# Placing F32R weight parts, activations and tiles at fixed distances from multiples of 256 bytes in SBUF

## The chip, the cores and the metric

The kernel runs on one core of a Trainium2 chip. The metric is the device time of one execution in microseconds; the time before is 1332.7 us, the median of 3 runs (1332.43 to 1333.14).

## The reference, cut to what matters

Two transformer blocks over 256 tokens of width 1024, all in float32.

```python
# block 1: adaLN modulation, top-k attention beside a short convolution, then PEER
mod = silu(c) @ w_ada + b_ada                    # shift1, scale1, gate1, shift2, scale2, gate2
h = rms_norm(x, norm1_w) * (1 + scale1) + shift1
proj = h @ w_in                                  # q k v | conv b c x | indexer q k w
y_mix = concat(rms_norm(dsa_attention(...)), rms_norm(short_conv(...)))
x = x + gate1 * (y_mix @ w_out)
h2 = rms_norm(x, norm2_w) * (1 + scale2) + shift2
# peer_ffn: 8 heads, 2 x 128 sub-keys, 16 of 16384 experts per head and token
a = gelu(einsum('qhkd,qd->qhk', peer_u[expert], h2))
x = x + gate2 * einsum('qhk,qhkd->qd', g * a, peer_v[expert])
# block 2, two layers: window attention and chunked gating, two gated branches, layer_norm
h = x @ w_in[l] + b_in[l]
merged = sigmoid(g_a) * (y_a @ w_branch_attn[l]) + sigmoid(g_g) * (y_g @ w_branch_gmlp[l])
x = layer_norm(ALPHA * x + merged @ w_out[l] + b_out[l], ln_g[l], ln_b[l])
```

## The kernel before

**Precision.** Most products are made of three F32R matmuls: an operand is split into a high part (a copy rounded to F32R) and a low part (what is left), and `mm3` (lines 245 to 248) adds high x high, high x low and low x high into one PSUM tile. `split` (lines 224 to 233) does it for a weight slab of 128 x 1024: ScalarE writes `wh` (L229), VectorE writes `wl` (L232). Slabs come with `load` (L219 to 222), 512 KB a DMA on the queue of SyncE. The slabs `w`, `wh`, `wl` have three buffers each, all in the pool `wpool`. Where plain F32 is enough, `load_any` puts a slab into any of these buffers and the matmul uses it whole.

**Stationary and streaming.** The first operand of a matmul is loaded as weights (PEld), the second streams (PE). In `mm_block` the weight slab is loaded and 256 columns of activations stream; in `mm_rows`, `rows_tile` and `v_mm` activations (or z parts) are loaded and 512 columns of the slab stream. Each matmul of the trace has a weight load of its own.

**Stages.** First stage: projections, attention and convolution, out projection, queries. U stage (`u_block`, 128 blocks): scores of all experts, each block 24 matmuls with `h2h`, `h2l`; the gelu goes into `Z`. Between the blocks a generator (`steps`) hands out the top-16 searches and then the `gates`, which build one-hot products in F16 and multiply `Z`; a budget of `STEP` = 1.45 per block sets how much of it is issued after each block. V stage (lines 1052 to 1080): for each of 128 slabs of `v`, `split_x` splits `Z[:, j]` into `zh`, `zl` (L241, L242), and `v_mm` (L1017) issues twelve matmuls of 512 columns into four PSUM tiles that stay open. At j = 80 `gate2_rows` makes eight small diagonal tiles `gdiag` (two buffers; L1038) that TensorE uses at L1039. Second block: `proj2` (24 matmuls of 256 columns with `xh4`, `xl4`), branch projections with `yh`, `yl`, rows with `mm_rows` and `rows_tile` (L1117), the latter from slabs split ahead into the buffers of sga, sgg, yh, yl (`wfirst`, `wlast`) or of ygT, yaT4.

**Order.** Each engine works its queue in order. Tiles are placed by stacks of pools: one grows from the low end of SBUF, a second, `using_default_side("right")`, from the high end (`gx`, later `xh4`, `xl4`). A tile is put right behind the one before it, at the next multiple of 32 bytes. In the program as built from the kernel before, these are the start addresses modulo 256 (each buffer of a tile has the same one):

| tile | start mod 256 |
|---|---|
| ident, the first tile of all | 128 |
| w, wh, wl | 160 |
| hh, hl (first stage) | 0 |
| h2h, h2l (U), Z, zh, zl (V), yh, yl, sga | 160 |
| xh4, xl4 | 224 |
| mh, ml, gx | 192 |

Slices in these tiles are whole multiples of 256 bytes apart (128 columns are 512 bytes), so a matmul's operands have the residue of their tiles.

Of the kernel before, what the change touches and what calls it, by code (L numbers as in the profile page):

```python
# [9 lines left out]
F32 = mybir.dt.float32  # L10
F32R = mybir.dt.float32r
F16 = mybir.dt.float16
# [7 lines left out]
P = 128  # L20
T = 256
D = 1024
# [9 lines left out]
BIG = -1e38  # L32
MARK = -3e38
WB = 3
EARLY = 2
STEP = 1.45
PRI = 300
# [124 lines left out]

def build(tc, d, out):
    nc = tc.nc
    ctx = ExitStack()
    V, S, G, TE = nc.vector, nc.scalar, nc.gpsimd, nc.tensor

    def pool(name, bufs, st=ctx, space=None):  # L170
        kw = {"reuse_waits": "tile"}
        if space is not None:
            kw["space"] = space
        return st.enter_context(tc.tile_pool(name=name, bufs=bufs, **kw))

    cst = pool("cst", 1)
    res = pool("res", 1)
    wpool = pool("wpool", 4)
    psm = pool("psm", 4, space=PSUM)


# [9 lines left out]
    def cc(name, i=0, n=1):  # L191
        o, w = COLS[name]
        return cols[:, o + i:o + i + n]
# [17 lines left out]
    def nm(s):  # L211
        uid[0] += 1
        return f"{s}_{uid[0]}"
# [3 lines left out]


    def load(src):  # L219
        w = wpool.tile([P, 1024], F32, tag="w", name=nm("w"), bufs=WB)  # L220
        nc.sync.dma_start(w, src)
        return w

    def split(w, hi=S, lo=V, dst=None):
        if dst is None:
            dst = [wpool.tile([P, 1024], F32R, tag=t, name=nm(t), bufs=3) for t in ("wh", "wl")]
        wh, wl = dst
        if hi is S:
            S.activation(wh, w, AF.Copy)  # L229
        else:  # L230
            hi.tensor_copy(wh, w)
        lo.tensor_sub(wl, w, wh.bitcast(F32))  # L232
        return wh, wl

    def split_x(pl, src, shape, name, hi=V, lo=V):
        xh = pl.tile(shape, F32R, tag=name + "h", name=nm(name + "h"))
        xl = pl.tile(shape, F32R, tag=name + "l", name=nm(name + "l"))
        if hi is S:
            S.activation(xh, src, AF.Copy)
        else:  # L240
            hi.tensor_copy(xh, src)  # L241
        lo.tensor_sub(xl, src, xh.bitcast(F32))  # L242
        return xh, xl
# [12 lines left out]

    def load_any(src, i):

        w = wpool.tile([P, 1024], (F32, F32R, F32R)[i], tag=("w", "wh", "wl")[i], name=nm("wn"), bufs=3)
        w = w if i == 0 else w.bitcast(F32)  # L260
        nc.sync.dma_start(w, src)
        return w
# [17 lines left out]
    def psum_mm():  # L280
        return psm.tile([P, 512], F32, tag="mm", name=nm("psmm"))
# [45 lines left out]
    st1 = ExitStack()  # L327
    psa = pool("psa1", 4, st1, PSUM)
    p1 = pool("p1", 1, st1)
    pw = pool("pw", 2, st1)  # L330
    adap = pool("adap", 5, st1)
    stg = ExitStack()
    with tc.using_default_side("right"):
        pg = pool("pg", 1, stg)
# [2 lines left out]
        return psa.tile([P, 512], F32, tag="aux", name=nm("aux"))  # L337

    xT = p1.tile([P, NCH, T], F32, name="xT")
    c1 = p1.tile([1, D], F32, name="c1")  # L340
    oc = ROWS["c"][0]
    nc.sync.dma_start(c1, d["rows"][0:1, oc:oc + D])
    xrow = p1.tile([P, 2, D], F32, tag="sq", name="xrow")
# [27 lines left out]
    def ada_col(dst, b, w, pl, crow):  # L371

        junk = pl.tile([P, D], F32, tag="junk", name=nm("junk"), bufs=1)
        V.scalar_tensor_tensor(junk, w, 0.5, crow, ALU.mult, ALU.mult, accum_out=dst)  # L374
        if b is not None:
            V.tensor_add(dst, dst, b)
# [25 lines left out]
    for k in range(NCH):  # L402
        ad = [ada_load(), ada_load()]
        wa = load(d["wa"][k])
        wb = p1.tile([P, D], F32, tag=("yaT", "ccT")[k % 2], name=nm("wb"))
        nc.sync.dma_start(wb, d["wb"][k])
# [14 lines left out]
        f, e = k == 0, k == NCH - 1  # L421
# [30 lines left out]
    def nload():  # L452
        w = load_any(d["w1"][wi[0]], wi[0] % 3)
        wi[0] += 1
        return w
# [19 lines left out]
    ada_step(5)  # L475


    iqT = p1.tile([P, 4, T], F32, name="iqT")
    for i in range(2):
        S.activation(iqT[:, 2 * i:2 * i + 2], iqp[i], AF.Copy)  # L480
    ikT = p1.tile([P, T], F32, name="ikT")
# [159 lines left out]
    for hp in range(4):  # L641
        ps = aux()
        for q in range(2):
            h = 2 * hp + q
# [17 lines left out]

    outp = []
    gx = pg.tile([P, NCH, T + 1], F32, name="gx")

    def out_half(half, y):

        for g in range(4):
            w = nload()
            if half == 0:  # L670
                ada_step(2)
                outp.append(psum_mm())
            for q in range(2):
                ps = outp[g][:, q * T:(q + 1) * T]
                for k in range(4):
                    sl = slice((4 * q + k) * P, (4 * q + k + 1) * P)
                    TE.matmul(ps, w[:, sl], y[:, k], start=half == 0 and q == 0 and k == 0, stop=half == 1 and k == 3,  # L677
                              skip_group_check=True)
            if half == 1:
                with tc.high_priority(offset=PRI):  # L680
                    for q in range(2):
                        n = 2 * g + q
                        V.scalar_tensor_tensor(x1T[:, n], outp[g][:, q * T:(q + 1) * T], gate1[:, n:n + 1], xT[:, n],
                                               ALU.mult, ALU.add)
                        S.activation(sq[:, n], x1T[:, n], AF.Square)
                        V.tensor_scalar(gx[:, n, :T], x1T[:, n], cw2[:, n:n + 1], None, ALU.mult)
# [39 lines left out]
    qps = []  # L726
    for s in range(EARLY):
        w = nload()
# [6 lines left out]
                        token_sum(ps2[:, :2], sq[:, n], n, NCH)  # L735
        qps.append(ps)
    powed = []
    rs2 = res.tile([P, T], F32, name="rs2")
    with tc.high_priority(offset=PRI):
        rs2p = rstd_bcast(pw, ps2[:, :2], D, EPS, aux, powed)  # L740
        V.tensor_copy(rs2, rs2p)
# [5 lines left out]
    Z = zp.tile([P, NJ, T], F32, name="Z")  # L747
# [55 lines left out]
    def retrieval_query(s):  # L803

        q2 = q2s[s % 3]
        if s < EARLY:
            qb = pu.tile([P, 1], F32, tag="qb", name=nm("qb"), bufs=2)
# [176 lines left out]
    for j in range(NJ):  # L984
# [3 lines left out]
        while budget > 0:  # L988
            c = next(todo, None)
# [6 lines left out]

    stv = ExitStack()
    psv = pool("psv", 1, stv, PSUM)
    pv = pool("pv", 3, stv)
    with tc.using_default_side("right"):  # L1000
        p4x = pool("p4x", 1)
    xr = x1T.rearrange("p k t -> p (k t)").rearrange("p (t d) -> p t d", t=2)
    xh4 = p4x.tile([P, NCH, T], F32R, name="xh4")
    xl4 = p4x.tile([P, NCH, T], F32R, name="xl4")

    acc = [psv.tile([P, 512], F32, name=f"vacc{i}") for i in range(4)]
    crow2 = pv.tile([P, D], F32, name="crow2", bufs=1)
# [5 lines left out]
    def v_mm(j, i, wh, wl, zh, zl):  # L1013

        ts_, sl = slice(i // 2 * P, (i // 2 + 1) * P), slice(i % 2 * 512, (i % 2 + 1) * 512)
        for n, (a, b) in enumerate(((zh, wh), (zh, wl), (zl, wh))):
            TE.matmul(acc[i], a[:, ts_], b[:, sl], start=j == 0 and n == 0, stop=j == NJ - 1 and n == 2)  # L1017

    def x1_rows():

        ps = [psum_mm() for _ in range(4)]
        for i in range(4):
            t, hf = i // 2, i % 2
            for q in range(4):
                TE.transpose(ps[i][:, q * P:(q + 1) * P], x1T[:, 4 * hf + q, t * P:(t + 1) * P], ident)
        for i in range(4):
            S.activation(xr[:, i // 2, i % 2 * 512:(i % 2 + 1) * 512], ps[i], AF.Copy)

    def gate2_rows():

        g2s = pv.tile([P, 8], F32, name="g2s", bufs=1)
        V.tensor_add(g2s, modB[:, 24:32], cc("bada", 40, 8))
        V.tensor_scalar(g2s, g2s, 1.0 / WSCALE, None, ALU.mult)
        for hf in range(2):
            ps = psum_mm()
            for q in range(4):
                dg = pv.tile([P, P], F32, tag="gdiag", name=nm("gdiag"), bufs=2)
                V.tensor_scalar(dg, ident, g2s[:, 4 * hf + q:4 * hf + q + 1], None, ALU.mult)  # L1038
                TE.matmul(ps[:, q * P:(q + 1) * P], ones, dg, start=True, stop=True)  # L1039
            S.activation(crow2[:, hf * 512:(hf + 1) * 512], ps, AF.Copy)  # L1040
# [11 lines left out]
    held = []  # L1052
    for j in range(NJ):
        if j % 8 == 4 and adai[0] < 48:
            ada_col(modB[:, adai[0] - 16:adai[0] - 15], None, load(d["ada"][adai[0]]), pv, crow2)
            adai[0] += 1
        w = load(d["v"][j])
        held.append(split(w) + split_x(pv, Z[:, j], [P, T], "z"))
        if j < NJ - VTAIL:
            for i in range(4):  # L1060
                v_mm(j, i, *held[-1])
            held.pop()
        if j == 16:
            x1_rows()
        if j == 80:
            gate2_rows()
    for i in range(4):
        for n, h in enumerate(held):
            v_mm(NJ - VTAIL + n, i, *h)
        t, sl = i // 2, slice(i % 2 * 512, (i % 2 + 1) * 512)  # L1070
# [14 lines left out]
    st4 = ExitStack()  # L1085
    psa = pool("psa4", 4, st4, PSUM)
    p4 = pool("p4", 1, st4)
    pq = pool("pq", 2, st4)
    w2i = [0]

    def next2():
        w = load(d["w2"][w2i[0]])
        w2i[0] += 1
        return w

    def split2(w, dst=None):
        return split(w, dst=dst)
# [36 lines left out]
    for l in range(2):  # L1134
        xh, xl = xh4, xl4
# [167 lines left out]
        for b in range(4):  # L1303
            ps = aux()
            for q in range(2):
                h = b + 4 * q
# [17 lines left out]
        for n in range(NCH):  # L1324
            wh, wl = split2(next2())
            pa = psum_mm()
            mm_block(pa[:, :T], wh, wl, yh, yl, n=4)
            pg = psum_mm()
# [74 lines left out]
```

## Time and profile before

| | |
|---|---|
| profiled execution | 1332.5 us |
| its span | 1330.3 us |
| PE busy | 1305.5 us, 98% |
| PEld busy | 1187.7 us, 89% |
| DVE busy | 1025.1 us, 77% |
| ACT busy | 631.0 us, 47% |
| DMA | 254.85 MB, mean 192 GB/s |

A matmul's busy time is from its start to its modelled end, and the next one starts well before that; the distance from start to start is what a matmul costs. In the chain of waits a piece of PE is exactly that distance. The granted clock is a share of full speed: 1.00 is 2.4 GHz.

### The profile page before, as it was taken

What the parts mean: (1) busy time and instruction counts of PE and PEld (TensorE: products, weight loads), DVE (VectorE), ACT (ScalarE), POOL (GpSimd) and SP (SyncE); (2) the same over time, 40 slices, a digit from 0 to 9 for tenths busy, and PEclk for the clock granted to TensorE, in tenths of its full rate; (3) what the DMA queues carried; (4) which work ended last, traced back from release to release, by engine and by line L of the source; (5) the groups of instructions that cost most, each with busy time, mean ns of one, the idle gap of its engine ahead of it and who ended that gap; (6) DMA issues with size and microseconds to landing.
All of it is one profiled execution on the core that took longest, in us unless ns stands there. A gap on an engine that the chain in (4) does not pass through costs nothing.

```text
span 1330.3 us, 23463 instructions
## 1 busy us (share of the span) xinstructions
PE 1305.5 (98%) x8968; PEld 1187.7 (89%) x8968; DVE 1025.1 (77%) x2159; ACT 631.0 (47%) x1100; POOL 21.1 (2%) x35
## 2 busy tenths in 40 slices
PE   7999999999999999999999999999989999999997
PEld 6868899999999999999888888888869999899996
DVE  7899399984688889885777777777784867868676
ACT  5535154644555544444443343343344754457642
POOL 1000000000000000000000000000010000000000
PEclk8999999999999999999999999999999999999999
DMA  9896244555544454545766776555665465554653
GB/s 369 317 345 233 84 144 150 167 191 187 172 165 159 148 167 147 173 158 187 224 202 218 216 221 201 180 191 194 196 232 160 142 222 187 189 174 140 209 191 111
DMA packets 72545, 254.85 MB, mean 192 GB/s; under 512 B 8305, under 2 KB 10481, under 8 KB 72178
## 3 DMA queue, kind: packets, MB, share of 16 engines
q1 hardware_dynamic: 72434, 253.36, 57.6%
q8 instruction: 71, 1.16, 0.3%
q14 instruction: 40, 0.33, 0.1%
HBM read 252.28 MB, written 1.05 MB: 190 GB/s over the span
## 4 chain that ended last, share of the span: by engine, by line
PE 88%; DVE 9%; ACT 1%; issue 1%; DMA 0%; DVEq 0%; POOL 0%; SPq 0%; POOLq 0%
PE vacc L1017 25%; PE psmm L246 15%; PE psmm L248 14%; PE psmm L247 14%; PE psmm L1117 3%; PE aux L955 2%; PE psmm L677 2%; DVE wl L232 2%; PE aux L443 2%; PE psmm L463 1%; PE iqp L443 1%; DVE Z L826 1%; PE aux L1207 1%; DVE junk L374 1%; PE psr L246 1%
## 5 line engine op out<-in xcount | busy, mean ns | idle before, releaser
L229 ACT ACTIVATE wh<-w 128x1024 fp32r<-128x1024 f32 x373 | 394.6, 1060 | 484.5 <-PE psmm L247 207.9
L232 DVE TENSOR_TENSOR wl<-w,wh 128x1024 fp32r<-128x1024 f32 x373 | 455.5, 1222 | 182.1 <-ACT wh L229 179.5
L246 PE MATMUL psmm<-h2h,wh 128*128 128x256 f32 x1136 | 327.7, 288 | 0.0
L248 PE MATMUL psmm<-h2h,wl 128*128 128x256 f32 x1136 | 322.4, 284 | 3.6 <-DVE wl L232 3.6
L247 PE MATMUL psmm<-h2l,wh 128*128 128x256 f32 x1136 | 321.0, 283 | 0.0
L248 PEld LDWEIGHTS psmm<-h2h,wl 128*128 128x128 f32 x1136 | 217.1, 191 | 5.8 <-DVE wl L232 5.5
L247 PEld LDWEIGHTS psmm<-h2l,wh 128*128 128x128 f32 x1136 | 217.3, 191 | 0.2 <-DVE h2l L774 0.2
L246 PEld LDWEIGHTS psmm<-h2h,wh 128*128 128x128 f32 x1136 | 217.1, 191 | 0.0
L1017 PE MATMUL vacc<-wh,zh 128*128 128x512 f32 x512 | 199.6, 390 | 0.0
L1017 PE MATMUL vacc<-wh,zl 128*128 128x512 f32 x512 | 199.5, 390 | 0.0
L1017 PE MATMUL vacc<-wl,zh 128*128 128x512 f32 x512 | 199.2, 389 | 0.0
L246 PE MATMUL psmm<-xh,wh 128*128 128x256 f32 x544 | 154.2, 283 | 0.0
L248 PE MATMUL psmm<-xh,wl 128*128 128x256 f32 x544 | 151.9, 279 | 0.0
L247 PE MATMUL psmm<-xl,wh 128*128 128x256 f32 x544 | 151.6, 279 | 0.0
L1017 PEld LDWEIGHTS vacc<-wh,zl 128*128 128x128 f32 x512 | 96.1, 188 | 20.1 <-DVE zl L242 0.2
L1017 PEld LDWEIGHTS vacc<-wl,zh 128*128 128x128 f32 x512 | 96.1, 188 | 19.8
L1017 PEld LDWEIGHTS vacc<-wh,zh 128*128 128x128 f32 x512 | 96.1, 188 | 19.8
L246 PEld LDWEIGHTS psmm<-xh,wh 128*128 128x128 f32 x544 | 102.1, 188 | 0.9 <-ACT yh L1316 0.3
L248 PEld LDWEIGHTS psmm<-xh,wl 128*128 128x128 f32 x544 | 102.2, 188 | 0.7 <-DVE mx L1218 0.7
L247 PEld LDWEIGHTS psmm<-xl,wh 128*128 128x128 f32 x544 | 101.9, 187 | 0.1
L242 DVE TENSOR_TENSOR zl<-Z,zh 128x256 fp32r<-128x256 f32 x128 | 54.6, 427 | 13.2 <-DVE zh L241 0.5
L947 DVE TENSOR_TENSOR oh<-iohr,ij 128x1024 f16<-128x1024 f16 x64 | 44.2, 693 | 22.8 <-PE aux L955 21.6
(388 smaller groups left out, 1732.0 us busy)
## 6 DMA issues: line engine op xcount, KB each, us to landing
w<-u SPq DMA_DIRECT2D x128, 512.0 KB, 3.3
w<-v SPq DMA_DIRECT2D x128, 512.0 KB, 4.2
w<-w SPq DMA_DIRECT2D x122, 512.0 KB, 3.8
ada<-ada SPq DMA_DIRECT2D x40, 512.0 KB, 6.1
wn<-w SPq DMA_DIRECT2D x23, 512.0 KB, 5.9
w<-wa SPq DMA_DIRECT2D x8, 512.0 KB, 7.5
wb<-wb SPq DMA_DIRECT2D x8, 512.0 KB, 4.8
w<-ada SPq DMA_DIRECT2D x8, 512.0 KB, 4.1
```

What stands on the lines that cost most here:

```text
L229: S.activation(wh, w, AF.Copy)
L232: lo.tensor_sub(wl, w, wh.bitcast(F32))
L242: lo.tensor_sub(xl, src, xh.bitcast(F32))
L246: TE.matmul(ps, sh, mh, start=first, stop=False)
L247: TE.matmul(ps, sh, ml, start=False, stop=False)
L248: return TE.matmul(ps, sl, mh, start=False, stop=last).ins
L443: TE.matmul(ps, st, mv, start=first, stop=e and part == 1, skip_group_check=True)
L677: TE.matmul(ps, w[:, sl], y[:, k], start=half == 0 and q == 0 and k == 0, stop=half == 1 and k == 3, skip_group_check=True)
L947: V.tensor_tensor(oh, bc(iohr.unsqueeze(1), [P, 4, P, 2]), bc(ij.unsqueeze(2), [P, 4, P, 2]), ALU.is_equal)
L955: TE.matmul(o, oh[:, i, :, q % 2], ow[:, i + r, :, q % 2], start=r == 0, stop=r == 1)
L1017: TE.matmul(acc[i], a[:, ts_], b[:, sl], start=j == 0 and n == 0, stop=j == NJ - 1 and n == 2)
L1117: last_mm[0] = TE.matmul(ps, x[:, k, ts_], slabs[k // 2][part][:, sl], start=k == 0 and r == 0 and i == 0, stop=k == NCH - 1 and r == 1).ins
```

## The change

Every SBUF pool is wrapped in `Lines`: a tile whose bytes per partition are no multiple of 256 is allocated with the next multiple and a view of it returned; tiles under 256 bytes of a pool that has `small` go to a pool of small tiles. `placed` opens two pools behind gaps of 64 and 128 bytes and a third gap of 64 behind them: `wh` goes to the first, `wl` to the second, three buffers each. The V stage gets two such pools for `zh` and `zl`. `edge` adds 96 bytes to a pool of the high side. Beside that, `c1` gets the buffer of `iqT`, `rs2` moves to the pool of `gx`, and `gdiag` has one buffer in place of two.

```diff
+LINE = 256
+HI_AT, LO_AT = 64, 192
+class Lines:
+    def edge(self):
+        self.pool.tile([P, 24], F32, name=self.name + "_edge")
+    def tile(self, shape, dtype, **kw):
+        size = 2 if dtype is F16 else 4
+        n = int(np.prod(shape[1:]))
+        if n * size % LINE == 0:
+            return self.pool.tile(shape, dtype, **kw)
+        if n * size < LINE and self.small is not None:
+            return self.small.tile(shape, dtype, **{"bufs": self.bufs, **kw})
+        t = self.pool.tile([shape[0], -(-n * size // LINE) * LINE // size], dtype, **kw)[:, :n]
...
+    def placed(name, st=ctx, bufs=3):
+        out, at = [], 0
+        for i, to in enumerate((HI_AT, LO_AT, 0)):
+            if (to - at) % LINE:
+                gap = st.enter_context(tc.tile_pool(name=f"{name}gap{i}", bufs=1))
+                gap.tile([P, (to - at) % LINE // 4], F32, name=f"{name}gap{i}")
+            at = to
+            if i < 2:
+                out.append(pool(f"{name}{i}", bufs, st))
+        return out
-    wpool = pool("wpool", 4)
+    wpool = pool("wpool", WB)
+    parts = placed("wpart")
-            dst = [wpool.tile([P, 1024], F32R, tag=t, name=nm(t), bufs=3) for t in ("wh", "wl")]
+            dst = [p.tile([P, 1024], F32R, tag=t, name=nm(t)) for p, t in zip(parts, ("wh", "wl"))]
-    def split_x(pl, src, shape, name, hi=V, lo=V):
-        xh = pl.tile(shape, F32R, tag=name + "h", name=nm(name + "h"))
-        xl = pl.tile(shape, F32R, tag=name + "l", name=nm(name + "l"))
+    def split_x(pls, src, shape, name, hi=V, lo=V):
+        xh = pls[0].tile(shape, F32R, tag=name + "h", name=nm(name + "h"))
+        xl = pls[1].tile(shape, F32R, tag=name + "l", name=nm(name + "l"))
+    p1.small = pw.small = pool("small", 1, st1).pool
-    c1 = p1.tile([1, D], F32, name="c1")
+    c1 = p1.tile([1, D], F32, tag="iqT", name="c1")
-    iqT = p1.tile([P, 4, T], F32, name="iqT")
+    iqT = p1.tile([P, 4, T], F32, tag="iqT", name="iqT")
+    pg.edge()
-    rs2 = res.tile([P, T], F32, name="rs2")
+    rs2 = pg.tile([P, T], F32, name="rs2")
-    pv = pool("pv", 3, stv)
+    pv = pool("pv", 2, stv)
+    pz = placed("z", stv)
+    p4x.edge()
-                dg = pv.tile([P, P], F32, tag="gdiag", name=nm("gdiag"), bufs=2)
+                dg = pv.tile([P, P], F32, tag="gdiag", name=nm("gdiag"), bufs=1)
-        held.append(split(w) + split_x(pv, Z[:, j], [P, T], "z"))
+        held.append(split(w) + split_x(pz, Z[:, j], [P, T], "z"))
+    p4.small = pq.small = pool("small4", 1, st4).pool
```

## Rows read from the trace of the kernel before

**Rows 1.** Page, part 1: busy time, share of the span, instructions.
```profile
PE 1305.5 (98%) x8968; PEld 1187.7 (89%) x8968; DVE 1025.1 (77%) x2159; ACT 631.0 (47%) x1100; POOL 21.1 (2%) x35
```
**Rows 2.** Page, part 4: the chain by engine.
```profile
PE 88%; DVE 9%; ACT 1%; issue 1%; DMA 0%; DVEq 0%; POOL 0%; SPq 0%; POOLq 0%
```
**Rows 3.** Table of stretches: busy PE, PEld, DVE, ACT, POOL; granted clock, DMA share, GB/s.
```profile
0.00:60.00 60.00, 53.30 (x293) 46.02 (x294) 50.34 (x99) 28.84 (x42) 4.10 (x11) 0.94 0.96 363
...
172.00:285.00 113.00, 109.37 (x889) 106.88 (x888) 112.25 (x478) 59.90 (x94) 0.00 (x0) 1.00 0.50 161
288.00:345.00 57.00, 57.00 (x478) 57.00 (x477) 26.95 (x25) 27.00 (x43) 0.00 (x0) 1.00 0.60 194
440.00:540.00 100.00, 100.00 (x936) 98.84 (x936) 89.55 (x168) 50.69 (x118) 0.00 (x0) 1.00 0.49 159
```
**Rows 4.** Chain, 310 to 312.6 us: start, us, what; first and last of 22.
```profile
309.98 0.12 PE psmm L248
...
312.50 0.12 PE psmm L248
```
**Rows 5.** Chain, 1191.5 to 1194.3 us; first and last of 25.
```profile
1191.43 0.12 PE psmm L248
...
1194.26 0.12 PE psmm L248
```
**Rows 6.** Chain, 1169.1 to 1171.8 us; first and last of 24 of 256 columns.
```profile
1169.14 0.12 PE psmm L246
...
1171.75 0.11 PE psmm L248
```
**Rows 7.** Chain of the whole execution: long pieces of PE.
```profile
137.51 14.25 PE psmm L677 x66
...
677.29 174.14 PE vacc L1017 x768
...
1143.99 11.20 PE psmm L1117 x48
```
**Rows 8.** Groups of weight loads, 288 to 345 us: count, busy us, mean ns, idle before.
```profile
L246 PEld LDWEIGHTS psmm<-h2h,wh 128*128 128x128 f32 x159 | 30.5, 192 | 0.0
```
**Rows 9.** Groups of weight loads, 1111 to 1143 us.
```profile
L246 PEld LDWEIGHTS psmm<-yh,wh 128*128 128x128 f32 x60 | 11.5, 192 | 0.0
```
**Rows 10.** Groups of weight loads, 1171 to 1185 us.
```profile
L246 PEld LDWEIGHTS psmm<-xh,wh 128*128 128x128 f32 x42 | 7.9, 188 | 0.0
```
**Rows 11.** Tile yh: count, ns least/median/most, first and last start.
```profile
L246 PE MATMUL psmm<-yh,wh x128: 277/283/290, 1109.6 to 1299.9; 128*128 128x256 f32 x128
```
**Rows 12.** Table of stretches, instructions with h2h (first two rows), with h2l (last two).
```profile
285.00:345.00 60.00, 60.00 (x335) 51.98 (x335) 0.00 (x0) 0.00 (x0) 1.00 0.59 193
345.00:629.00 284.00, 265.36 (x1393) 220.47 (x1391) 0.00 (x0) 0.00 (x0) 1.00 0.50 162
...
285.00:345.00 60.00, 47.14 (x168) 32.02 (x167) 0.00 (x0) 1.00 0.59 193
345.00:629.00 284.00, 196.50 (x696) 132.95 (x696) 0.00 (x0) 1.00 0.50 162
```
**Rows 13.** Instructions of DVE in order, 440 to 447 us: start, us.
```profile
440.98 0.69 DVE L947 TENSOR_TENSOR oh<-iohr,ij 128x1024 f16<-128x1024 f16 x1 [0.39 <-PE aux L955]
441.59 1.22 DVE L232 TENSOR_TENSOR wl<-w,wh 128x1024 fp32r<-128x1024 f32 x1
...
444.38 0.69 DVE L947 TENSOR_TENSOR oh<-iohr,ij 128x1024 f16<-128x1024 f16 x1 [0.38 <-PE aux L955]
```
**Rows 14.** Page, part 5: matmuls of xh in the second block.
```profile
L246 PE MATMUL psmm<-xh,wh 128*128 128x256 f32 x544 | 154.2, 283 | 0.0
```
**Rows 15.** Groups of matmuls, 1169.5 to 1185 us.
```profile
L246 PE MATMUL psmm<-xh,wh 128*128 128x256 f32 x47 | 13.0, 276 | 0.0
```
**Rows 16.** Instructions in order, 849 to 857 us: gdiag and its matmuls.
```profile
851.97 0.48 DVE L1038 TENSOR_SCALAR gdiag<-ident,g2s 128x128 f32<-128x128 f32 x2
...
852.30 0.52 PEld L1039 LDWEIGHTS psmm<-gdiag,ones 128*128 128x128 f32 x4 [0.40 <-DVE gdiag L1038]
```

More of the change, by code (lines that the diff above doesn't have):

```diff
@@ L159, in layout, with __init__ @@
     return a
+class Lines:
+    def __init__(self, pool, name, bufs):
+        self.pool, self.name, self.bufs, self.small = pool, name, bufs, None
+    def edge(self):
[8 more added lines that the diff above has]
+        t = self.pool.tile([shape[0], -(-n * size // LINE) * LINE // size], dtype, **kw)[:, :n]
+        return t if len(shape) == 2 else t.rearrange("p (a b) -> p a b", a=shape[1]) if len(shape) == 3 else \
+            t.rearrange("p (a b c) -> p a b c", a=shape[1], b=shape[2])
 def build(tc, d, out):
@@ L173, in pool @@
             kw["space"] = space
-        return st.enter_context(tc.tile_pool(name=name, bufs=bufs, **kw))
+        p = st.enter_context(tc.tile_pool(name=name, bufs=bufs, **kw))
+        return p if space is not None else Lines(p, name, bufs)
+    def placed(name, st=ctx, bufs=3):
[8 more added lines that the diff above has]
+        return out
     cst = pool("cst", 1)
     res = pool("res", 1)
-    wpool = pool("wpool", 4)
+    wpool = pool("wpool", WB)
+    parts = placed("wpart")
     psm = pool("psm", 4, space=PSUM)
@@ L219, in load @@
     def load(src):
-        w = wpool.tile([P, 1024], F32, tag="w", name=nm("w"), bufs=WB)
+        w = wpool.tile([P, 1024], F32, tag="w", name=nm("w"))
         nc.sync.dma_start(w, src)
@@ L257, in load_any @@
     def load_any(src, i):
-        w = wpool.tile([P, 1024], (F32, F32R, F32R)[i], tag=("w", "wh", "wl")[i], name=nm("wn"), bufs=3)
+        w = (wpool, *parts)[i].tile([P, 1024], (F32, F32R, F32R)[i], tag=("w", "wh", "wl")[i], name=nm("wn"))
         w = w if i == 0 else w.bitcast(F32)
```

## The prediction

> **What bounds the kernel now.** The page's head and part 1 come first: the profiled execution took 1332.5 us, its span is 1330.3 us, and TensorE's 1305.5 us busy are 98% of that [rows 1]. 2.2 us lie outside the span, and the median of the runs shown is 1332.7 us, so sums made against 1332.5 us hold for the median too. Busy time overlaps for pipelined matmuls, so the chain (part 4) is the better witness: 88% of it is PE, 9% DVE [rows 2]. Next, the table of stretches shows where the DVE part lies. From 172 to 285 us DVE is busy 112.25 of 113.00 us: the top-16 searches set the pace there, and a faster matmul gives nothing. From 285 us on PE has no idle time, while DVE is busy 26.95 of 57.00 us right after, and 89.55 of 100.00 us among the gates [rows 3]. From 172 us on the granted clock is 1.00 in these rows, the upper level of 2.4 GHz, so the clock is not what differs below.
>
> Last, the chain in close-up gives the spacing of matmuls, start to start. Each has its own weight load, which runs beside the matmul before it. A matmul of 256 columns takes:
> - 120.0 ns in the U stage (309.98 to 312.50 us, 21 steps, 2.52 us) [rows 4];
> - 117.9 ns in the second block (1191.43 to 1194.26 us, 24 steps, 2.83 us) [rows 5];
> - 113.5 ns in the same second block some 20 us earlier (1169.14 to 1171.75 us, 23 steps, 2.61 us) [rows 6].
>
> Of 512 columns: 226.7 ns in the V stage (174.14 us for 768), 233.5 ns where rows of the second block are made (11.20 us for 48). And one pass of a plain F32 matmul of 256 columns, some twice as long as one in F32R, takes 215.9 ns (14.25 us for 66) [rows 7]. I take half of that, 108.0 ns, as an estimate of 256 F32R columns with no disturbance, and 215.9 ns of 512. So every F32R matmul here loses 5 to 18 ns.
>
> Why placement is a candidate: call offset the distance, modulo 256, between where the streaming operand starts and where the weights loaded meanwhile start. In the program before, U has its activations (moving) and its weight parts both 160 bytes past a multiple of 256, offset 0. The second block's xh4 and xl4 are at 224 with weights at 160, offset 64. V has offset 0 again, rows of the second block 32. The same pair of spacing and weight-load time returns with the offset: offset 0 at 256 columns has loads of 192 ns in U and in the branch projections of yh, yl [rows 8, 9], offset 64 has 188 ns [rows 10]. The matmuls of yh, yl have a median of 283 ns, and U's in that stretch are paced at 120.0 ns with the same loads [rows 4, 11], so I take 120.0 ns for both. Rows 5 and 6 are the warning: one set of addresses, two spacings, so a run of matmuls can also settle in one of two rhythms.
>
> **The change, part by part.** All differences below count from the first tile; that one starts 128 past a multiple of 256 in the program before, so the title's 0, 64 and 192 are 128, 192 and 64 in absolute terms, with the same differences.
>
> *U stage.* Moving 0, weights 64 or 192: the offset becomes 64 on either side, that of the second block. 335 + 1393 matmuls with h2h and 168 + 696 with h2l lie after 285 us [rows 12]: 2592. I take the better level, 113.5 ns, since the new starts are whole multiples of 64 where the old ones were 32 off: 2592 x 6.5 ns = 16.8 us. Bounds: 108.0 ns gives 31.1 us, 117.9 ns gives 5.4 us, 120.0 ns nothing. DVE covers it: a block among the gates takes 3.40 us (from one oh, at 440.98 us, to the next, at 444.38) [rows 13], and DVE works 0.8955 of that stretch, 3.04 us [rows 3]. The new block takes 3.40 - 24 x 0.0065 = 3.24 us, so 0.20 us remain; at 108.0 ns it would be 3.11 us and the cover all but gone.
>
> *Second block.* xh4, xl4: 3 x 544 matmuls [rows 14], of which some 139 have 113.5 ns already (47 of the first kind in that stretch, and as many or one fewer of the two others) [rows 15]; 1493 x 4.4 ns = 6.6 us (bounds: nothing; at 108.0 ns 15.5 us). yh, yl: 3 x 128 [rows 11] x 6.5 ns = 2.5 us (bounds 0 and 4.6). Rows from the slabs `wfirst`, `wlast` and the slab pair of `ahead` in p4: weights and slab now both at 0, V's offset; 168 matmuls by the loops (192 less the 24 on wh, wl) x (233.5 - 226.7) = 1.1 us. The rows on wh and wl keep an offset of 64 at 512 columns, which no row shows alone; I cost them at nothing.
>
> *V stage.* zh with wh, zl with wl and zh with wh again are what meets: each pair has offset 0, as before. I take no change; the bounds are 215.9 ns (1536 x 10.8 = 16.6 us less) and 233.5 ns (10.4 us more).
>
> *First stage and DVE stretch.* In the first 60 us the DMA engines are 0.96 busy, so loads decide, not matmuls; the plain F32 passes after it define the undisturbed 215.9 ns and have nothing to win back; from 172 to 285 us DVE decides [rows 3, 7]. Nothing.
>
> *Single buffer of gdiag.* They are made in pairs now, and PE waits 0.40 us for a pair [rows 16]. With one buffer each of the eight waits on DVE for the matmul before it, and behind it in DVE's queue stands the low-part subtraction of the next V block (1.22 us in rows 13), for which PE then waits. Six more waits of 0.40 us are 2.4 us; with a subtraction ahead of each, 6 x 1.22 = 7.3 us; and none where vacc matmuls fill in. I take 2.4 us, the row's.
>
> *The rest* moves tiles: rs2 to the pool of gx, c1 shares iqT's buffer (c1 is read before the loop of the first stage, iqT is written after it), small tiles go to a pool of their own, z parts keep three buffers. No instruction is added, and SP's queue issues the same loads. If a new overlay made a tile wait at a stage's start, that would be some us; the pools open in the same order over the same stages, so nothing is charged.
>
> Sum: 16.8 + 6.6 + 2.5 + 1.1 - 2.4 = 24.6 us. 1332.5 - 24.6 = 1307.9 us.
>
> **The rivals.**
> 1. *Only the other rhythm.* U and yh, yl get 117.9 ns, the usual level of offset 64: 2976 x 2.1 ns = 6.2, slabs 1.1, gdiag -2.4, so 4.9 us less: 1327.6 us. For it: most of the second block's matmuls run so (the first kind lasts 283 ns in the mean over all, 276 ns in the quick stretch) [rows 14, 15]. Against: their starts are 32 off a multiple of 64.
> 2. *Placement does nothing*, and the levels come from something else that differs between stages: 1332.5 + 2.4 = 1334.9 us. For it: rows 5 and 6. Against: 120.0 and 192 ns return together in two far-apart stages with offset 0. The Trainium skill (TensorE: Matmul & The Clock Gate, Step-by-step: what each phase is for) says that TensorE has two independent SBUF read ports and that loading the next weights takes no read bandwidth from a running matmul. By that rule this rival would be the outcome. The trace does not agree with it as it stands: matmuls of the same shape and with loads of the same size are spaced 113.5, 117.9 and 120.0 ns.
> 3. *V pays (slower).* With starts on multiples of 64 the two streams of V meet head on, where they now lie half a step off, and each V matmul takes the 233.5 ns of the slowest 512-column row: +10.4 us. With rival 1's gain of 4.9 us it decides from 3.2 ns per V matmul on; with the forecast gain from 16 ns. With U between 117.9 and 120.0 ns: 1332.5 + 10.4 + 2.4 less 0 to 7.3 = 1338.0 to 1345.3 us, say 1342. For it: 512 columns are what reacts most to offset (226.7 against 233.5). Against: V's offset is not changed.
> 4. *More than forecast.* The disturbance goes altogether: 31.1 + 15.5 + 4.6 + 16.6 + 3.0 (slabs at 215.9) - 2.4 = 68.4, so 1264.1 us; halfway there from the forecast is 1286. For it: nothing in the trace says that 113.5 ns is a floor. Against: no F32R matmul with its own load shows a steady 108.0 or 215.9 ns.
>
> **How the numbers follow.** Forecast 0.43 (its own range 1298 to 1318), rival 1 0.17, rival 2 0.10, rival 3 0.12, rival 4 0.18. A change of under 0.2% (2.7 us) can't be told from none here. Faster: 0.43 + 0.17 + 0.18 = 0.78; same: rival 2, 0.10; slower: rival 3, 0.12. The range 1280 to 1335 holds the forecast, rivals 1 and 2 and rather more than half of rival 4 (0.43 + 0.17 + 0.10 + 0.10): 0.80.
>
> **What would show it.** Steps of a U block at 113 to 114 ns and loads of 188 ns between 285 us and the end of U; about 17 us less from there to the first vacc matmul; the second block's projections all at 113.5 ns; V's 768 matmuls again at 226.7 ns each. U at 118 ns means rival 1, at 120 rival 2, V above 227 rival 3, U near 108 with PE waiting for wl or DVE among the gates rival 4. The prediction is wrong if V moves by more than 5 ns either way, or if gdiag or a stage's start costs over 5 us.

## The result and the profile after

The changed kernel takes 1316.7 us (median of 4 runs, 1314.99 to 1318.93), the kernel before beside it 1332.6 us (4 runs, 1332.07 to 1333.14): a ratio of 0.9882, 95% interval [0.9865, 0.9899]. It is faster by 15.8 us where 24.6 us were forecast. The profiled execution took 1316.85 us, its span is 1314.3 us, 16.0 us shorter than before.

The page of the changed kernel, part 1 and the first line of part 4, as in [rows 1, 2]:

```profile
PE 1286.9 (98%) x8968; PEld 1161.2 (88%) x8968; DVE 1024.1 (78%) x2159; ACT 629.9 (48%) x1100; POOL 21.5 (2%) x35
...
PE 80%; DVE 15%; ACT 2%; issue 2%; DMA 1%; POOL 0%; SPq 0%; DVEq 0%; ACTq 0%; POOLq 0%
```

The same 8968 matmuls, and PE is 18.6 us less busy. DVE's part of the chain grew from 9% to 15%, from 115 to 191 us. 64 us of that lie ahead of 285 us, where PE and DVE wait for each other in turn and the chain now follows the other of two branches; those stages take as long as before. The other 12 us stand between the two layers of the second block, where PE now waits (below). The stretches, columns as in [rows 3]:

```profile
172.00:285.00 113.00, 107.17 (x892) 103.52 (x891) 112.25 (x477) 59.41 (x93) 0.00 (x0) 1.00 0.50 161
288.00:345.00 57.00, 57.00 (x506) 57.00 (x505) 28.73 (x32) 29.55 (x46) 0.00 (x0) 1.00 0.62 202
440.00:540.00 100.00, 100.00 (x966) 99.05 (x966) 92.61 (x171) 51.98 (x123) 0.00 (x0) 1.00 0.50 163
```

57 us hold 506 matmuls instead of 478, 100 us among the gates 966 instead of 936, at the same granted clock of 1.00 (2.4 GHz). DVE is busy 112.25 of the first 113 us as before, and now 92.61 of 100 us among the gates. (Two of a count had begun before its stretch; below, a spacing from a count leaves them out: 57.00 us over 504 are 113.1 ns, over 476 119.7.) Next the chain of the changed kernel in a U block without gates (first and last of 25 steps), to be held against [rows 4], and its weight loads, against [rows 8]:

```profile
295.97 0.11 PE psmm L285
...
298.69 0.11 PE psmm L285
```
```profile
L284 PEld LDWEIGHTS psmm<-h2h,wh 128*128 128x128 f32 x168 | 31.5, 188 | 0.0
```

24 steps in 2.72 us are 113.3 ns (120.0 before); a load takes 188 ns (192 before). The matmuls of yh follow, as in [rows 11]: all within 2 ns, 276 ns instead of 283.

```profile
L284 PE MATMUL psmm<-yh,wh x128: 275/276/277, 1098.1 to 1284.4; 128*128 128x256 f32 x128
```

The chain of the changed kernel among the gates, one block from its first matmul to the next block's first:

```profile
440.00 0.17 PE psmm L284
440.17 0.12 PE psmm L285
...
440.76 0.11 PE psmm L284
...
442.80 0.47 PE aux L995 x8
443.28 0.17 PE psmm L284
```

The block takes 3.28 us (3.40 before). Behind the eight gate matmuls (L995) the first step takes 0.17 us, the next five 118 ns each (440.17 to 440.76), and only then come 18 at 113.3 ns (to 442.80). The gain is not had at once.

The long pieces of the chain of the changed kernel, as in [rows 7]:

```profile
137.04 14.25 PE psmm L717 x66
...
663.33 177.49 PE vacc L1059 x768
```

V's 768 matmuls take 177.49 us instead of 174.14, so 231.1 ns each instead of 226.7. PE's instructions in V show how (start, duration):

```profile
700.13 0.40 PE L1059 MATMUL vacc<-wl,zh 128*128 128x512 f32 x1
700.37 0.40 PE L1059 MATMUL vacc<-wh,zl 128*128 128x512 f32 x1
700.60 0.39 PE L1059 MATMUL vacc<-wh,zh 128*128 128x512 f32 x1
700.83 0.39 PE L1059 MATMUL vacc<-wl,zh 128*128 128x512 f32 x1
701.06 0.39 PE L1059 MATMUL vacc<-wh,zl 128*128 128x512 f32 x1
701.28 0.40 PE L1059 MATMUL vacc<-wh,zh 128*128 128x512 f32 x1
701.52 0.40 PE L1059 MATMUL vacc<-wl,zh 128*128 128x512 f32 x1
```

The starts are 0.24, 0.23, 0.23, 0.23, 0.22, 0.24 us apart and repeat: a pattern of six, where the kernel before has an even 0.227. And the stretch of gdiag, chain of the changed kernel:

```profile
840.82 0.22 PE psmm L1081 x2
841.04 0.69 PE vacc L1059 x3
841.73 0.46 PE psmm L1081 x2
```

Between two of the small matmuls of `gdiag`, V's own matmuls now fill in; PE doesn't stand still.

Stage by stage, in us, from starts of first and last matmuls in both traces (with 0.6 us between U and V in both, the columns add up to the two spans). Blocks are counted from 0, from the first 24 matmuls with h2h on; the first 14 make queries. The step from layer 1 to layer 2 is taken up to the first matmul on `wa_ygT`:

| stage | before | after | difference | forecast |
|---|---|---|---|---|
| up to U's 34th block (DVE sets the pace) | 284.4 | 283.8 | -0.6 | 0 |
| U, blocks 34 to 58, no gates | 69.4 | 65.7 | -3.8 | |
| U, the rest, gates between blocks | 275.0 | 264.5 | -10.5 | |
| U after 284 us together | 344.4 | 330.2 | -14.2 | -16.8 |
| V with gdiag | 353.8 | 360.2 | +6.3 | +2.4 |
| projections (xh, xl) and first rows, both layers | 238.3 | 232.8 | -5.5 | -6.6 and part of -1.1 |
| yh, yl, both layers | 46.1 | 43.5 | -2.6 | -2.5 |
| rows at the ends of both layers | 44.3 | 43.5 | -0.8 | the other part of -1.1 |
| from layer 1 to layer 2, and from V to the block | 10.5 | 11.9 | +1.4 | 0 |
| tail behind PE | 7.8 | 7.8 | 0.0 | 0 |

The row +1.4 is a wait that the earlier matmuls ran into. DVE in the changed kernel, at the start of layer 2, in order:

```profile
1141.39 1.41 DVE L1417 SCALAR_TENSOR_TENSOR x1T<-x1T,rvy,fin 128x512 f32<-128x512 f32 x2
1142.72 1.22 DVE L270 TENSOR_TENSOR wl<-w,wh 128x1024 fp32r<-128x1024 f32 x1
1143.85 1.22 DVE L270 TENSOR_TENSOR wa_yaT<-w,wa_ygT 128x1024 fp32r<-128x1024 f32 x1
...
1145.59 0.68 DVE L1175 TENSOR_TENSOR xl<-aux,xh 128x512 fp32r<-128x512 f32 x1
```

PE's instructions there that waited (in brackets for how long, and for what):

```profile
1142.28 1.29 PE L1171 MATMUL aux<-ident,x1T 128*128 128x128 f32 x8 [0.31 <-DVE x1T L1417]
...
1146.33 1.20 PE L1160 MATMUL psmm<-wh,xl 128*128 128x512 f32 x4 [0.60 <-DVE xl L1175]
```

DVE's layer normalisation and the two slab splits behind it take as long as before; PE arrives sooner, waits 0.31 us for x1T, and 0.60 us for an xl that stands behind both splits. The chain of the changed kernel goes on backwards from there through splits and loads of slabs: from 1117 to 1138 us it holds three loads of 3.3 to 4.2 us, ScalarE and VectorE, and not PE. In the kernel before, the transposes of x1T (L1128) started without a wait:

```profile
1155.03 1.03 PE L1128 MATMUL aux<-ident,x1T 128*128 128x128 f32 x8
```

### The profile page after: what moved, and what is told of

The parts are those of the page before. It is cut to its first block, busy times and chain, and to the rows that moved or that the text cites. A ratio compares the mean times of both kernels' runs of the same rounds, so it can differ in the third digit from the quotient of the medians.

```text
span 1314.3 us, 23462 instructions
## 1 busy us (share of the span) xinstructions
PE 1286.9 (98%) x8968; PEld 1161.2 (88%) x8968; DVE 1024.1 (78%) x2159; ACT 629.9 (48%) x1100; POOL 21.5 (2%) x35
## 4 chain that ended last, share of the span: by engine, by line
PE 80%; DVE 15%; ACT 2%; issue 2%; DMA 1%; POOL 0%; SPq 0%; DVEq 0%; ACTq 0%; POOLq 0%
PE vacc L1059 26%; PE psmm L284 14%; PE psmm L286 13%; PE psmm L285 13%; DVE wl L270 3%; PE psmm L1160 2%; PE aux L995 2%; PE psmm L717 2%; DVE junk L413 2%; PE psmm L502 1%; DVE Z L866 1%; DMA w<-w 1%; DVE Z L864 1%; DVE Z L863 1%; DVE wbl L459 1%
## 5 line engine op out<-in xcount | busy, mean ns | idle before, releaser
L286 PE MATMUL psmm<-h2h,wl 128*128 128x256 f32 x1136 | 316.7, 279 | 5.3 <-DVE wl L270 5.0
L284 PE MATMUL psmm<-h2h,wh 128*128 128x256 f32 x1136 | 321.3, 283 | 0.0
L285 PE MATMUL psmm<-h2l,wh 128*128 128x256 f32 x1136 | 314.9, 277 | 0.1
L286 PEld LDWEIGHTS psmm<-h2h,wl 128*128 128x128 f32 x1136 | 213.3, 188 | 8.5 <-DVE wl L270 8.4
L285 PEld LDWEIGHTS psmm<-h2l,wh 128*128 128x128 f32 x1136 | 213.7, 188 | 0.3 <-DVE h2l L814 0.2
L284 PEld LDWEIGHTS psmm<-h2h,wh 128*128 128x128 f32 x1136 | 213.4, 188 | 0.0
L1059 PE MATMUL vacc<-wl,zh 128*128 128x512 f32 x512 | 202.7, 396 | 0.0
```

What stands on the lines that cost most here:

```text
L284: TE.matmul(ps, sh, mh, start=first, stop=False)
L285: TE.matmul(ps, sh, ml, start=False, stop=False)
L286: return TE.matmul(ps, sl, mh, start=False, stop=last).ins
```

## Experiments

Unless a diff says more, each kernel is the changed one with other values for the places of the parts (a `placed` with `hi` and `lo` is that of the experiment with z parts at 0). An offset is the place of what is loaded less the place of what streams, modulo 256. U's 256-column matmuls stream from place 0, so the place of a weight part is its offset; in V the weight parts stream and the z parts are loaded. Ratios are to the kernel before, measured beside each.

**All parts at one place, 64.** Is V's loss due to two places for high and low parts?

```diff
-HI_AT, LO_AT = 64, 192
+HI_AT, LO_AT = 64, 64
```

> The changed kernel with both weight parts and both z parts at 64 (192 becomes 64): every pair in V keeps offset 0, but streaming operands of successive matmuls all start at the same place, and all starts stay whole multiples of 64. U keeps an offset of 64, always to the same side. Theory 'jump' (V lost its 5 ns per matmul because wh and wl start 128 apart): V back at 226.7 ns, 2.72 us per slab against 2.77, so 6.5 us less than the changed kernel, about 1310 us. Theory 'half line' (V lost because its starts are no longer 32 past a multiple of 64): V stays at 231 ns or above, about 1317 us. Both: U at 113.3 ns if the side of the offset does not count; up to 117.9 ns (+10 us) if it does.

1310.6 us (1309.53 to 1312.32), ratio 0.9834 [0.9818, 0.9851]; span 1308.8 us. The long V piece and the stretches of U (columns as in [rows 3]) of this kernel:

```profile
661.65 174.12 PE vacc L1059 x768
```
```profile
288.00:345.00 57.00, 57.00 (x505) 57.00 (x505) 28.73 (x30) 29.61 (x46) 0.00 (x0) 1.00 0.60 203
440.00:540.00 100.00, 100.00 (x972) 99.04 (x971) 93.08 (x172) 52.29 (x123) 0.00 (x0) 1.00 0.47 163
```

V is back at 226.7 ns: two places for high and low parts cost V 4.4 ns per matmul. The whole V stage takes 354.0 us against 360.2 with two places. U without gates is as with two places. Among the gates it is a little faster (972 matmuls against 966), because one step of 118 ns follows the first step of a block where the changed kernel has five:

```profile
440.18 0.12 PE psmm L285
440.30 0.11 PE psmm L286
```

The second block is 1.5 us longer than with two places; why is open. This is the fastest version of all that ran.

**All parts at 0.** Everything of the change but the offset: rounded sizes, one gdiag buffer, moved tiles.

```diff
+HI_AT, LO_AT = 0, 0
```

> The changed kernel with weights and z parts at 0 as the activations: offset 0 in U, V and the second block, all starts whole multiples of 64, no jump. Theory 'offset' (U gained because the offset became 64): U and the second block's projections back at 120 ns, loads of 192 ns; with V at 226.7 ns the sum is 1317 + 17 + 8 - 7 = about 1335 us. Theory 'half line' (U gained because starts became multiples of 64): U stays at 113.3 ns, V at 231 ns, 1317 us.

1337.0 us (1336.24 to 1337.45), ratio 1.0031 [1.0019, 1.0044]; span 1334.3 us. Its chain at the place of [rows 4], and its U without gates:

```profile
309.89 0.12 PE psmm L285
...
312.53 0.12 PE psmm L286
```
```profile
288.00:345.00 57.00, 57.00 (x477) 57.00 (x476) 26.61 (x25) 26.20 (x41) 0.00 (x0) 1.00 0.55 192
```

22 steps in 2.64 us: 120.0 ns again, with loads of 192 ns, U as long as before. V with its single gdiag takes 353.7 us, 353.8 before: the buffer costs nothing. The second block is 4.0 us longer than before (343.2 against 339.2 us), because its projections lose the offset that they had, 64 to the other side. So rounding, multiples of 64 as such and the moved tiles bring nothing without the offset.

The Trainium skill (TensorE: Matmul & The Clock Gate, Step-by-step: what each phase is for) has two independent read ports, so that a weight load takes no read bandwidth from the running matmul. This kernel and the one with all parts at 64 differ in the start addresses alone, and by 26.4 us of time and 6.7 ns per matmul of U: if the two took nothing from each other, their places could not matter so, and here the measurement decides. Which of the two waits, and where, no run shows.

**Z parts at 0, weight parts at 64 and 192.** Does V need its offset of 0 as well?

```diff
-    def placed(name, st=ctx, bufs=3):
+    def placed(name, st=ctx, bufs=3, hi=HI_AT, lo=LO_AT):
-        for i, to in enumerate((HI_AT, LO_AT, 0)):
+        for i, to in enumerate((hi, lo, 0)):
-    pz = placed("z", stv)
+    pz = placed("z", stv, hi=0, lo=0)
```

> The changed kernel with the z parts at 0 in place of 64 and 192: V's offset is 64 to one side or the other, as for the rows made with wh and wl (230 to 231 ns). U untouched, 113.3 ns. Offset theory: V at 230 to 231 ns, within 2 us of the changed kernel, 1315 to 1317 us; if an offset of 64 helped 512 columns as it helps 256, V would be at 220 ns, 1300 us.

1315.6 us (1315.10 to 1316.21), ratio 0.9873 [0.9857, 0.9890]. The V piece:

```profile
662.92 176.92 PE vacc L1059 x768
```

230.4 ns. With offsets of 64 and -64 in place of 0, V is no slower than in the changed kernel.

**Z parts crossed: 192 and 64 against 64 and 192.** Every pair at 128 as the prediction pairs them (what streams, and the next matmul's load), starts still changing.

```diff
-    pz = placed("z", stv, hi=0, lo=0)
+    pz = placed("z", stv, hi=192, lo=64)
```

> The changed kernel with the z parts crossed (zh at 192, zl at 64): each load in V then starts 128 from the slab that streams meanwhile, half of 256, the farthest it can be. If distance is what counts in V, it is the best here: towards 216 ns, 1296 us; if 0 is the best distance for 512 columns, V gets the 235 ns of its worst step in each, 6 us more than the changed kernel, 1323 us. U untouched.

1315.1 us (1313.68 to 1315.31), ratio 0.9865 [0.9848, 0.9881]. The V piece:

```profile
663.18 175.81 PE vacc L1059 x768
```

228.9 ns: a little better than the changed kernel, worse than constant places with offset 0.

**Weight parts at 64, z parts at 192.** Offset 128 in V without a change of start.

```diff
+HI_AT, LO_AT = 64, 64
+    pz = placed("z", stv, hi=192, lo=192)
```

> The kernel with all parts at 64, but both z parts at 192: in V the load starts 128 from the streaming slab, and there is no jump between matmuls. U and the second block untouched, 113.3 ns. If 0 is the best distance for 512 columns (226.7 ns), V gets slower: crossed parts gave 228.8 ns with jumps, so 228 to 230 ns and 1313 to 1316 us. If a distance helps 512 columns as it helped 256 (one disturbance of two gone), V would be at 220 ns and the time at 1300 us.

1318.7 us in one run (1333.7 before beside it). The V piece:

```profile
662.60 178.45 PE vacc L1059 x768
```

**Weight parts at 64, z parts at 128.** Offset 64 in V, the one that U likes.

```diff
+HI_AT, LO_AT = 64, 64
+    pz = placed("z", stv, hi=128, lo=128)
```

> The kernel with all parts at 64, but both z parts at 128: in V the load starts 64 behind the start of the streaming slab (the other side from rows made with wh and wl in the kernel with all parts at 64, which take 225.8 to 231.7 ns, 229 in the mean). 0 is best for 512 columns: 229 ns, 1314 us. A distance helps: 220 ns, 1300 us. U untouched.

1320.9 us in one run. The V piece:

```profile
662.66 179.20 PE vacc L1059 x768
```

232.4 ns at offset 128 and 233.3 at 64, without any change of start. So an offset other than 0 costs V time by itself; and at 512 columns the offset of 64 is the worst that ran, at 256 columns the best. 233.3 is also what [rows 7] give for rows of the second block: 11.20 us for 48.

The side counts. In the 48 matmuls of `mm_rows`, mh and ml are loaded from place 0 and `wh`, `wl` stream. With all parts at 64 that is offset -64, with all parts at 192 (below) 64. First and last of the 48, in this order:

```profile
1114.70 0.39 PE L284 MATMUL psr<-wh,mh 128*128 128x512 f32 x1
...
1125.45 0.39 PE L286 MATMUL psr<-wh,ml 128*128 128x512 f32 x1
```
```profile
1124.84 0.40 PE L284 MATMUL psr<-wh,mh 128*128 128x512 f32 x1
...
1135.81 0.40 PE L286 MATMUL psr<-wh,ml 128*128 128x512 f32 x1
```

47 steps in 10.75 us are 228.7 ns at -64, in 10.97 us 233.4 ns at 64.

These prices bear on what V lost in the changed kernel. With the z parts at 0, slabs at 64, 192, 64 stream in turn: two steps at -64 and one at 64, by these prices (2 x 228.7 + 233.4) / 3 = 230.3 ns. 230.4 were measured, so there a change of start costs nothing of its own. And the crossed parts, every pair at 128 by the prediction's pairing, should then take at least the 232.4 ns of a constant 128; they take 228.9. Another pairing fits better. If what counts is the load for the matmul after next, the changed kernel has offsets 128, 128, 0 in turn, (2 x 232.4 + 226.7) / 3 = 230.5 ns (231.1 measured), and the crossed parts 0, 0, 128, 228.6 ns (228.9 measured). This reading was found after the runs and no run was made to test it; that a changing start costs time by itself is not shown either.

**All parts at 128.** Would any offset other than 0 do for U?

```diff
+HI_AT, LO_AT = 128, 128
```

> The kernel with all weight and z parts at 128: U's offset becomes 128, half of 256; V keeps offset 0 without a jump, 226.7 ns. If any offset but 0 does, U at 113.3 ns and the time at 1310 to 1311 us. If the offset must be 64, U lies between 113.3 and 120 ns: up to 16 us more.

1333.9 us in one run (1333.7 before). Its U without gates:

```profile
288.00:345.00 57.00, 57.00 (x483) 57.00 (x482) 26.90 (x25) 27.42 (x41) 0.00 (x0) 1.00 0.63 195
```

57.00 us over 481 matmuls are 118.5 ns, with uneven steps: not the quick rhythm.

**All parts at 192.** The other side, offset -64, alone.

```diff
+HI_AT, LO_AT = 192, 192
```

> The kernel with all weight and z parts at 192: U's offset is 64 to the other side than with all parts at 64, the side that the second block had before the change, where both 113.5 and 117.9 ns were seen; V 226.7 ns. If the side does not count: U at 113.3 ns, 1310 to 1311 us. If this side has two rhythms by itself, part of the U blocks at 117.9 ns: 1315 to 1320 us.

1325.2 us in one run. Its stretches, and its chain among the gates (19 steps, then the gate matmuls):

```profile
288.00:345.00 57.00, 57.00 (x505) 57.00 (x504) 28.83 (x29) 29.97 (x46) 0.00 (x0) 1.00 0.64 204
440.00:540.00 100.00, 100.00 (x943) 98.84 (x942) 89.92 (x169) 50.26 (x118) 0.00 (x0) 1.00 0.50 161
```
```profile
439.90 0.12 PE psmm L286
...
442.14 0.47 PE aux L995 x8
```

At -64, U reaches 113.3 ns where nothing interrupts it, but among the gates it stays at 117.9 ns (2.24 us for 19). These are the levels of [rows 5, 6], at the same offset: one set of addresses, and which rhythm comes goes with what ran just before. Behind the first step of a block the quick one returns after one step with all parts at 64, and after five with 64 and 192 in turn.

**224 of 256 columns.** Is 113.3 ns set by the streaming or by the weight loads? From the version with all parts at 64; most of the sums for the last 32 tokens are left out.

```diff
+COLUMNS = 224
-            i = mm3(ps, wh[:, sl], wl[:, sl], xh[:, xoff + k], xl[:, xoff + k], k == 0, k == n - 1)
+            if k == 0:
+                i = mm3(ps, wh[:, sl], wl[:, sl], xh[:, xoff + k], xl[:, xoff + k], k == 0, k == n - 1)
+            else:
+                i = mm3(ps[:, :COLUMNS], wh[:, sl], wl[:, sl], xh[:, xoff + k, :COLUMNS], xl[:, xoff + k, :COLUMNS],
+                        False, k == n - 1)
```

> The kernel with all parts at 64; the matmuls of U, of the projections and branches stream 224 of 256 columns, except the first three of each PSUM tile (32 tokens' share of the sums is left out there). What is 113.3 ns made of? If the streaming sets it (108 ns of the estimate and a disturbance), it falls with the columns, 32/256 of 106.7 ns = 13 ns, to 100 ns, and U blocks without gates take 2.45 us or less. If the weight load sets it (one load after the other, each started when the matmul before starts), it stays at 113.3 ns or a little under, and the blocks at 2.7 us.

1355.3 us in one run: its time doesn't answer the question, for PE, DVE and ACT wait for each other between 230 and 312 us in an order of instructions that came out otherwise, 28 us in all (blocks 14 to 34 take 93.1 us against 65.2 with all parts at 64). A stretch that is free of this does:

```profile
318.00:348.00 30.00, 30.00 (x269) 30.00 (x269) 13.49 (x11) 14.94 (x23) 0.00 (x0) 1.00 0.62 193
```

30.00 us over 267 matmuls are 112.4 ns, where 57.00 over 503 were 113.3 with all columns; and blocks 34 to 58 take 65.12 us instead of 65.63, 1.0 ns for each of 24 x 21 shortened matmuls. An eighth of the streaming would be 13.5 ns of the 108.0 taken from [rows 7]. So the quick rhythm does not follow the columns. That the weight load sets it is the likeliest of what is left, but it is not shown: no run has another load, and the steps at 224 columns are uneven (103 to 123 ns), as in a disturbed rhythm. The Trainium skill (TensorE: Matmul & The Clock Gate, LDWEIGHTS (loading the stationary operand)) gives P / 1.2 ns for a load, for 128 columns an estimate of 106.7 ns by that page. The 112.4 ns from start to start at 224 columns are near to it, though a load lasts 188 to 192 ns in the records.

**Offsets alone.** The kernel before, with gaps that give each pair in U and the second block an offset of 64 and V one of 0; sizes not rounded, two gdiag buffers, starts 32 past multiples of 64 as before.

```diff
+    def gap(n, st=ctx):
+        pool(f"gap{len(gaps)}", 1, st).tile([P, n // 4], F32, name=f"gap{len(gaps)}")
+        gaps.append(n)
+    gap(64)
+    parts = pool("parts", 3)
+    gap(192)
-            dst = [wpool.tile([P, 1024], F32R, tag=t, name=nm(t), bufs=3) for t in ("wh", "wl")]
+            dst = [parts.tile([P, 1024], F32R, tag=t, name=nm(t)) for t in ("wh", "wl")]
...
+    gap(32, stv)
+    pz = pool("pz", 3, stv)
+    p4x.tile([P, 16], F32, name="p4x_edge")
```

> The kernel before, with gaps only: both weight parts 64 further on (224, activations and z as before at 160), z parts moved to 224, and 64 bytes behind xh4 and xl4 so that they start at 160. No tile is rounded to 256, none starts at a multiple of 64, gdiag keeps two buffers. If only the offset between stream and load counts, this does all that the kernel with all parts at 64 does: U and the second block at 113.3 ns, V at 226.7 ns, 1310 to 1312 us. If starts at multiples of 64 matter too, U stays above 113.3 ns: 117.9 ns would give about 1323 us.

1319.3 us (1319.09 to 1319.44), ratio 0.9892 [0.9875, 0.9908]. Its stretches:

```profile
288.00:345.00 57.00, 57.00 (x505) 57.00 (x505) 28.85 (x30) 30.22 (x46) 0.00 (x0) 1.00 0.64 204
440.00:540.00 100.00, 100.00 (x957) 98.93 (x956) 91.18 (x171) 51.58 (x120) 0.00 (x0) 1.00 0.50 159
```

The offset alone brings most of it, and 113.3 ns where nothing interrupts. Among the gates (957 against 972 with all parts at 64) and in the second block (matmuls of yh of 281 ns instead of 276) it drops to the other rhythm more often: of blocks 60 to 129, 35 settle at 113 ns and 35 at 118, where with all parts at 64 all 70 settle at 113. The version with all parts at 64 is 8.7 us faster, 7.7 us by the two ratios. That much lies in the rest of the change, given the offset: in starts at whole multiples of 64 or in the rounded and moved tiles, which no run separates; some 1 us of it is rows of 512 columns, which keep an offset of 32 or -32 here.

**All parts at 32, and all at 96.** How wide is the good stretch of offsets?

```diff
+HI_AT, LO_AT = 32, 32
```

> All parts of the weights start 32 bytes past a multiple of 256, moving activations and z parts at 0 as before: offset 32 in U and in the second block, no change of start from one weight tile to the next, offset 0 in V. Theory A (the quick rhythm belongs to a small stretch of offsets around 64, and 32 lies inside it): blocks 34 to 58 at 113.3 ns, V 2.720 us a slab, time about 1310 to 1314. Theory B (the rhythm falls by steps with the offset, half way at 32): spacing 115 to 118 ns, time 1318 to 1327. Theory C (only a start at a multiple of 64 has it): 119 to 120 ns and about 1333 to 1337, as with all parts at 0. I hold A .3, B .4, C .3. V is 226.7 ns by all three.

```diff
+HI_AT, LO_AT = 96, 96
```

> All parts of the weights start 96 bytes past a multiple of 256, activations and z parts at 0: offset 96. Theory A (stretch around 64, 96 inside): 113.3 ns in blocks 34 to 58 and about 1310 to 1314 in all. Theory B (by steps, half way between the 113.3 of 64 and the 119 to 120 of 128): 115 to 118 ns, 1318 to 1327. Theory C (multiples of 64 alone): 119 to 120 ns, about 1333. I hold A .3, B .4, C .3. V 226.7 ns by all three, since its z parts and its activations keep one start.

(The z parts lie with the weight parts in both, at 32 and at 96, not at 0; V's offset is 0 as stated.) 1330.2 us for both (1328.96 to 1332.13 and 1328.37 to 1332.40), ratios 0.9981 [0.9971, 0.9990] and 0.9982 [0.9972, 0.9992]. The U stretch at 32, then at 96:

```profile
288.00:345.00 57.00, 57.00 (x484) 57.00 (x484) 26.90 (x25) 27.57 (x42) 0.00 (x0) 1.00 0.62 194
```
```profile
288.00:345.00 57.00, 57.00 (x488) 57.00 (x487) 27.33 (x26) 27.94 (x43) 0.00 (x0) 1.00 0.63 199
```

118.3 and 117.3 ns (most steps lie between 115 and 122), little better than 0 and like 128. In spacing this is the case of steps, in time it is nearer to the case that only a multiple of 64 has it: none of my three numbers for the time held. V takes 226.7 ns in both. The good places are single ones: of the six offsets that ran, 64 and, where nothing interrupts, -64.

## Why the prediction was right, and where its sizes were off

- **U.** The step held: the offset of 64 gives the better level, 113.3 ns where 113.5 was taken, with loads of 188 ns. Of 16.8 us, 14.2 came. The term took every one of 2592 matmuls from 120.0 ns to the better level; among the gates the first of a block doesn't gain, and the next five run at 118 ns, as they did before. The 75 blocks from 58 to 133 gained 9.0 us, or 0.12 us each, where 24 x 6.5 ns = 0.16 were forecast. DVE was cover enough: it is busy 92.61 of 100 us there, and no wait of PE for `wl` appears from 290 us to the end of U.
- **V.** This is the term that was mis-sized: 0 taken, +6.3 us measured. The step that failed is "each pair has offset 0, as before", taken to settle it. Which load meets which stream was assumed, not read from a row, and two places for high and low parts make that matter. One place for both removes the whole loss; whether the change of start or another pairing causes it is open (see the experiment with z parts at 128). Rival 3 had the right place and over half the size (6.3 us, 10.4 in the rival), but not its cause: with starts at multiples of 64 and one place, V takes 226.7 ns. V above 227 ns was named as rival 3's sign, so the outcome is the forecast in U and part of rival 3 in V; at 4.4 ns V stayed just under the 5 ns at which the prediction called itself wrong.
- **gdiag.** +2.4 us taken, nothing measured: of the three cases named, V's matmuls fill in. That is luck for the number: without this charge the forecast would have been 27.0 us, further from the 15.8.
- **xh, xl.** 6.6 forecast, 5.5 measured together with the rows at the start of a layer. **yh, yl** 2.5, measured 2.6. The projections have a median step of 113 ns, but a mean of 115.5 (118.8 before), so the sign "all at 113.5" failed. The slabs' rows at the layers' ends came to 0.8 of 1.1. Two readings in that term were off: 11.20 us for 48 are 233.3 ns, not 233.5, and 36 of the matmuls, not 24, lie on `wh` and `wl`, as three of the four slabs of `ahead` do; the term stays near 1 us. **Nothing for the rest** held except between the layers, where PE ran into DVE and gave back 1.4 us.
- Added up: 14.2 + 5.5 + 2.6 + 0.8 + 0.6 - 6.3 - 1.4 = 16.0 us of span.
- **Rivals.** Rival 1 (only the other rhythm) is what offset -64 does among the gates, not what 64 and 192 together did. Rival 2 fell with all parts at 0. Rival 4 did not come, and an eighth fewer columns bought only 1.0 ns per matmul.

What stays open: why 64 suits 256 columns and 0 suits 512; what in two places costs V 4.4 ns; why +64 settles after the gates and -64 doesn't; and what holds the quick rhythm at 113.3 ns. The runs show which addresses do it, not what in the chip does. U's activations at two places, and another size of weight load, were not tried.

## What to carry to other kernels

Where PE is the bound, read the spacing from start to start in the chain, per shape, and compare stages; if equal shapes differ at the same granted clock, look at the start addresses modulo 256 of what streams and what is loaded meanwhile, and try them one shape at a time, because the best offset for one shape was the worst for another. Where streaming operands take turns in one run of matmuls, try one place for all of them first: it was the fastest here. And when a spacing is multiplied by a count, look at what happens just behind each interruption: the quick rhythm may take some matmuls to come back, or not come back at all.

## What the runs showed of the hardware that was not expected

- F32R matmuls of 256 columns, each with its own load, in U without gates: 120.0 ns at offset 0, 113.3 at 64 and at -64, 117.3 to 118.5 with uneven steps at 32, 96 and 128.
- Of 512 columns, in V: 226.7 ns at offset 0 with one start, wherever that lies (0, 32, 64, 96, 128 and 192 ran); 233.3 at 64, 232.4 at 128, and 228.7 at -64 (rows of the second block); with slabs at 64 and 192 in turn 231.1 (z parts with them), 230.4 (z parts at 0) and 228.9 (z parts crossed).
- An eighth fewer streaming columns saves 1.0 of 113.3 ns per matmul in U without gates.
- One number in the change, the place of the low parts, is worth 6 us: 1310.6 us with all parts at 64.
